# Weight tiles moved by 64 bytes, three loads on another queue, and another order at the end of an encoder block

## The chip, the cores and the metric

The kernel runs on one core of one Trainium2 chip. The metric is the device time of one execution in microseconds (us). TensorE multiplies matrices; VectorE (DVE), ScalarE (ACT) and GpSimd (POOL) work on elements; SyncE (SP) only issues transfers. A PEld row is the load of TensorE's stationary operand, which overlaps the matmul before it.

## The reference

One layer of an encoder on 256 tokens of width 2048, all in float32:

```python
h = _rmsnorm(x, norm1_g)
proj = h @ w_in                      # q: 1536, k: 512, v: 512, u: 512 columns
a = _rmsnorm(_window_attention(q, k, v, sink), attn_out_g)   # 12 heads, 4 kv heads, |t-s| <= 128
f = _rmsnorm(_fourier_mix(u, w_fourier), fourier_out_g)      # Re(DFT2) per group, then a linear map
x = x + jnp.concatenate([a, f], axis=-1) @ w_out
x = x + _conv_ffn(_rmsnorm(x, norm2_g), w_up, dw_w, dw_b, w_down)
return _rmsnorm(x, normf_g)

def _conv_ffn(h, w_up, dw_w, dw_b, w_down):                  # D_FF = 5504
    up = h @ w_up
    gate, val = up[..., :D_FF], up[..., D_FF:]
    gate = depthwise_conv_3(gate, dw_w) + dw_b
    return (jax.nn.gelu(gate, approximate=False) * val) @ w_down
```

## The kernel before

**Products in three parts.** Every large product is computed from numbers split in two: `hi` is the operand rounded to the type float32r, `lo` is what the rounding left. A product is hi x hi + hi x lo + lo x hi, each a float32r matmul that adds into the same PSUM bank. Weights come from memory whole, as units of 128 partitions x 2048 numbers (1 MB), into `raw`; ScalarE makes `hi` from it (L143) and VectorE makes `lo` (L144). `raw`, `hi` and `lo` have three buffers each, used in turn.

**Two kinds of unit.** In `moving_weights` (L282 to L284) the activations are the stationary operand and the weights move, 512 columns at a time: activation-high with `hi`, activation-low with `hi`, activation-high with `lo`. It is used for u and v (`ps_u`, `ps_v`), the output projection (`ps_a`, `ps_ff`) and the down-projection (`ps_d`, and `ps_e` for the last group). One unit has 24 such matmuls. In `still_weights` (L293, L294) the weights are stationary: a block of `hi` meets the tokens' high and low parts together (512 columns), and a block of `lo` the high parts alone (256 columns). It is used for q and k (16 units) and for the up-projection (`ps_gate`, `ps_val`, 86 units). One unit has 16 such pairs.

**The order.** The program is an order written out by hand. u comes first, then v, q and k with the attention of earlier heads woven in, the output projection, and then the feed-forward part: groups of eight up units (four gate, four value), with a group of four down units behind each but the first. `step(i)` splits the unit two ahead while unit i is multiplied; a split ends by issuing the load of the unit three ahead on SP's queue, where it waits until its `raw` buffer is free.

**Where the tiles lie.** A tile begins at the same byte of every partition. By the sizes of the tiles in the pools, in the order in which they are made, the tokens' parts (`hT`, later `hU`) begin at bytes that are 96 modulo 512; `raw`, `hi` and `lo` (8192 bytes each) at 288; `cat` and `act`, the activations of the output and down products, at 288; the attention's `v_hi` and `v_lo` at 448 and its `pt` at 192. A block of 128 stationary columns is 512 bytes of a partition, and all offsets within these tiles are multiples of 512, so these residues hold for every operand.

**The start.** Tokens come transposed as eight tiles `xT`. SP issues the loads in order: the first 256 columns of tokens, the first quarter of weight unit 0, the next 256 columns, the second quarter, the next 512 columns, the third and fourth quarter, and so on (L168 for tokens, L121 for weights). ScalarE's queue issues only the small `vec` (L176), which the first conversion of tokens (L235, then L236 on VectorE) needs too.

**The end.** The last down group has three blocks and is done product by product (`ps_e`): column block c of four, row block b of two. `last_post` adds a product to the running sum `xs` on VectorE (L833), squares it on ScalarE with a running total (L819) and, for c below 3, multiplies it by the final gain on POOL (L836). When all four of a row block are there, `most_of` and `last_scale` form its scale (VectorE L843, L845, L850; POOL L854), and `finish` writes four outputs: c = 0 and 1 on ScalarE (L869), c = 3 (L863) and c = 2 (L867) on VectorE, each with an output transfer on SP's queue (L870). The last product (3, 1) is done in two halves of 256 columns (L941 to L943); `most_of` of row block 1 stands between them.

Of the kernel before, what the change touches and what calls it, by code (L numbers as in the profile page):

```python
# [8 lines left out]
F32 = mybir.dt.float32  # L9
F32R = mybir.dt.float32r  # L10
AF = mybir.ActivationFunctionType
ALU = mybir.AluOpType

P = 128
D = 2048
S = 256
# [36 lines left out]
FF_GROUPS = [list(range(g * 4, min(g * 4 + 4, NF))) for g in range((NF + 3) // 4)]  # L53
# [3 lines left out]
def block_kernel(  # L57
# [17 lines left out]
    nc = tc.nc  # L75
# [3 lines left out]
    wp = ctx.enter_context(tc.tile_pool(name="wp", bufs=1))  # L79
# [3 lines left out]
    def f32(ap):  # L83
        return ap.bitcast(F32)

    def bank(pool, name):
        return pool.tile([P, 512], F32, tag=pool.name, name=name)
# [24 lines left out]
    raws, halves = {}, {}  # L112

    def load(i, pieces=1):
        if i < len(units) and i not in raws:
            src, n = units[i]
            raws[i] = wp.tile([P, 2048], F32, tag="raw", name=f"raw{i}", bufs=RAW)
            m = n // pieces
            for p in range(pieces):
                s = slice(p * m, (p + 1) * m)  # L120
                nc.sync.dma_start(raws[i][:, s], src[:, s])  # L121
                yield
# [6 lines left out]
    def split_parts(i, pieces):  # L129
        if i >= len(units):  # L130
            return
        n = units[i][1]
        raw = raws[i]
        hi = wp.tile([P, 2048], F32R, tag="hi", name=f"hi{i}", bufs=3)
        lo = wp.tile([P, 2048], F32R, tag="lo", name=f"lo{i}", bufs=3)
        halves[i] = (hi, lo)
        m = n // pieces
        for p in range(pieces):
            s = slice(p * m, (p + 1) * m)
            if i == 0 and p == 0:  # L140
                nc.vector.tensor_copy(hi[:, s], raw[:, s])
            else:
                nc.scalar.activation(hi[:, s], raw[:, s], AF.Copy)  # L143
            nc.vector.tensor_tensor(lo[:, s], raw[:, s], f32(hi[:, s]), ALU.subtract)  # L144
            yield
        for _ in load(i + RAW):
            pass
        load_more(i + RAW)
# [8 lines left out]
    xTc = [cat_pool.tile([P, 512], F32, tag="cat", name=f"xT{c}") for c in range(8)]  # L157
# [6 lines left out]
    rel = cat_pool.tile([P, 512], F32, tag="cat", name="rel")  # L164
    xs = [base.tile([P, 2, 512], F32, tag=f"xs{c}", name=f"xs{c}") for c in range(4)]

    def load_x(c, o=0, n=512):
        nc.sync.dma_start(xTc[c][:, o : o + n], xT[:, c * 512 + o : c * 512 + o + n])  # L168


    warm = base.tile([P, 2], F32, tag="warm", name="warm")
# [2 lines left out]

    first = load(0, 4)
    nc.scalar.dma_start(vec[:, 0:NK], vecs[:, 0:NK])  # L176
    load_x(0, 0, S)
    next(first)
    load_x(0, S, S)
    next(first)  # L180
    load_x(1)
    next(first)
    next(first)
    load_x(2)
    second = load(1, 4)
    next(second)
# [16 lines left out]
    def load_more(i):  # L203

        if i == 4:
            for c in range(2):
                nc.sync.dma_start(xs[c], x[:, :, c * 512 : (c + 1) * 512])
        if i == 5:
            for c in range(2, 4):
                nc.sync.dma_start(xs[c], x[:, :, c * 512 : (c + 1) * 512])  # L210
        if i == 6:
            nc.sync.dma_start(chan, c_chan)
            nc.sync.dma_start(wfs, wf)
            nc.sync.dma_start(pos, c_pos)
        if i == 7:
            nc.sync.dma_start(vec[:, NK:V_N], vecs[:, NK:V_N])
            nc.sync.dma_start(rel, c_rel)
# [8 lines left out]
    ps = bank(dn, "ps_warm")  # L226
# [49 lines left out]
    def moving_weights(hi, lo, n, kk, act, b, ps, first, last, q0=0):  # L276

        for q, k in enumerate(kk, q0):
            ah = act(k)[:, b * P : (b + 1) * P]
            al = act(k)[:, S + b * P : S + (b + 1) * P]  # L280
            wh, wl = hi[:, q * n : (q + 1) * n], lo[:, q * n : (q + 1) * n]
            nc.tensor.matmul(ps, ah, wh, start=first and q == q0, stop=False)  # L282
            nc.tensor.matmul(ps, al, wh, start=False, stop=False)  # L283
            nc.tensor.matmul(  # L284
                ps, ah, wl, start=False, stop=last and q == q0 + len(kk) - 1
            )
# [18 lines left out]
    def step(i, ahead=2):  # L305
        todo, later[:] = list(later), []
        for g in todo:
            next(g, None)
        split(i + ahead)
        for g in todo:  # L310
            for _ in g:
                pass
# [24 lines left out]
    for k in range(NK):  # L337
        c, q = k // 4, k % 4
# [4 lines left out]
        hi, lo = halves[c]  # L343
# [392 lines left out]
    for n, (c, kq) in enumerate(OUT_ORDER):  # L736
        i = N_OUT + n
# [14 lines left out]
        if kq >= 2:  # L752
            part = "a" if kq == 2 else "f"
            ps = ps_a[c] if kq < 3 else ps_a[c, "f"]
            last = c in added
# [15 lines left out]
    gfb = fp.tile([P, D], F32, tag="gfb", name="gfb", bufs=1)  # L771
    nc.gpsimd.dma_start(gfb, normf_g.partition_broadcast(P))
    hT[:] = hT2
    act = {}
# [49 lines left out]
    def down_post(g, c, ps):  # L824
# [2 lines left out]
            nc.vector.tensor_tensor(xb, ps[b], xb, ALU.add)  # L827
        yield

    def last_post(c, b, ps, o=0, n=512, part=None):  # L830

        xb = xs[c][:, b, o : o + n]
        nc.vector.tensor_tensor(xb, ps, xb, ALU.add)  # L833
        square_sum(c, b, c if part is None else part, o, n)
        if c < 3:
            nc.gpsimd.tensor_tensor(  # L836
                xb, xb, gfb[:, c * 512 + o : c * 512 + o + n], ALU.mult
            )

    def most_of(b, n):  # L840

        tot = base.tile([P, 1], F32, tag=f"tot3{b}", name=f"tot3{b}")
        nc.vector.tensor_reduce(tot, ssq3[:, b, 0:n], mybir.AxisListType.X, ALU.add)  # L843
        var = base.tile([P, 1], F32, tag=f"part3{b}", name=f"part3{b}")
        nc.vector.tensor_scalar(var, tot, 1.0 / D, EPS, ALU.mult, ALU.add)  # L845
        return var

    def last_scale(b, n, var):
        v = base.tile([P, 1], F32, tag=f"var3{b}", name=f"var3{b}")
        nc.vector.scalar_tensor_tensor(  # L850
            v, ssq3[:, b, n : n + 1], 1.0 / D, var, ALU.mult, ALU.add
        )
        r = base.tile([P, 1], F32, tag=f"rstd3{b}", name=f"rstd3{b}")
        nc.gpsimd.tensor_tensor(r, v, half_pow[:, 0:1], ALU.pow)  # L854
        return r

    def finish(b, r):
        y = [
            fp.tile([P, 512], F32, tag="act", name=f"y{b}{c}", bufs=12) for c in range(4)
        ]  # L860
        for c in (0, 3, 1, 2):
            if c == 3:
                nc.vector.scalar_tensor_tensor(  # L863
                    y[c], xs[c][:, b, :], r, gfb[:, 1536:2048], ALU.mult, ALU.mult
                )
            elif c == 2:
                nc.vector.tensor_scalar(y[c], xs[c][:, b, :], r, None, ALU.mult)  # L867
            else:
                nc.scalar.activation(y[c], xs[c][:, b, :], AF.Copy, scale=r)  # L869
            nc.sync.dma_start(  # L870
                out[b * P : (b + 1) * P, c * 512 : (c + 1) * 512], y[c]
            )

    last = len(FF_GROUPS) - 1
    n = 0
    while n < len(ff_units):
        kind, g, j = ff_units[n]
        i = n_front + n
        if n == 0:
            pair = []  # L880
            for q in range(2):
                ps = bank(mm, f"ps_{ff_units[q][0]}{j}")
# [16 lines left out]
        hi, lo = halves.pop(i)  # L899
        if kind == "down" and g == last:  # L900
            break
        if kind == "down":
            ps = [bank(dn, f"ps_d{g}{j}{b}") for b in range(2)]
# [4 lines left out]
        else:  # L908
            ps = bank(mm, f"ps_{kind}{j}")
# [4 lines left out]


    halves[i] = (hi, lo)
    todo = []
    for c, b in [(0, 0), (0, 1), (1, 0), (1, 1), (2, 0), (3, 0), (2, 1), (3, 1)]:
        hi, lo = halves[i + c]
        ps = bank(dn, f"ps_e{c}{b}")  # L920
        if (c, b) != (3, 1):
            moving_weights(hi, lo, 512, FF_GROUPS[last], act.get, b, ps, True, True)
            todo.append((last_post, (c, b, ps)))
        if (c, b) in [(0, 1), (1, 0)]:
            step(i + c)
        if (c, b) != (0, 0):
            for f, a in todo:
                f(*a)
            todo = []
        if (c, b) == (3, 0):  # L930
            r3 = last_scale(0, 3, most_of(0, 3))
        if (c, b) == (2, 1):
            finish(0, r3)
    for p in range(2):
        ps = bank(dn, f"ps_e31{p}")
        for q, k in enumerate(FF_GROUPS[last]):
            o = q * 512 + p * 256
            ah, al = act[k][:, P:S], act[k][:, S + P : 2 * S]
            wh, wl = hi[:, o : o + 256], lo[:, o : o + 256]
            end = q == len(FF_GROUPS[last]) - 1  # L940
            nc.tensor.matmul(ps[:, 0:256], ah, wh, start=q == 0, stop=False)  # L941
            nc.tensor.matmul(ps[:, 0:256], al, wh, start=False, stop=False)
            nc.tensor.matmul(ps[:, 0:256], ah, wl, start=False, stop=end)  # L943
        last_post(3, 1, ps[:, 0:256], p * 256, 256, 3 + p)
        if p == 0:
            var = most_of(1, 4)
    finish(1, last_scale(1, 4, var))


def _layout(inp):  # L950
# [90 lines left out]
```

## Time and profile before

| What | Value |
|---|---|
| Median of three runs | 990.43 us (990.28 to 990.92) |
| The profiled execution | 989.97 us |
| Its span, first to last instruction | 988.2 us |
| TensorE busy with matmuls | 977.0 us, 5185 matmuls |
| VectorE, ScalarE busy | 696.1 and 466.5 us |
| First and last matmul of the program's own work | start 4.80 and 978.58 us |
| Bytes moved | 186.42 MB, mean 189 GB/s |

A row of the timeline has start, duration, engine, line, operation, output and inputs, shape and count; in brackets stands how long the engine was idle before it and what ended that. A row of groups ends with the busy time in us, the mean duration in ns, and the idle time before. Matmuls are pipelined: a matmul's own duration is longer than the time to the start of the next, so paces are read from starts.

### The profile page before, as it was taken

How to read it: one execution, taken by the hardware profiler on the slowest of the kernel's cores; microseconds unless marked ns; L12 is line 12 of the kernel's file. 1: busy time of each engine (PE TensorE's matmuls, PEld its weight loads, DVE VectorE, ACT ScalarE, POOL GpSimd, SP SyncE). 2: the span in 40 equal slices, each digit the busy share in tenths (PEclk: the TensorE clock that was granted, in tenths of full speed). 3: DMA queues.
4: the chain of work that ended last, by engine and by line, in shares of the span. 5: the costliest groups of instructions: out<-in, count | busy, mean ns of one | idle time of the engine just before them, and what ended most of it. 6: DMA issues, size and time to landing. Idle time of an engine off the chain costs nothing.

```text
span 988.2 us, 12858 instructions
## 1 busy us (share of the span) xinstructions
PE 977.0 (99%) x5185; PEld 838.2 (85%) x5185; DVE 696.1 (70%) x935; ACT 466.5 (47%) x587; POOL 23.6 (2%) x35
## 2 busy tenths in 40 slices
PE   9999999999999999999999999999999999999996
PEld 7788898888888888888888888888888888888885
DVE  6658877575687776767767767777677677676764
ACT  6756666544454434444434444344344343443434
POOL 0000000000000000000000000000000000000003
PEclk9999999999999999999999999999999999999999
DMA  9844443445545555464555555555545455555542
GB/s 330 341 178 153 148 165 134 171 170 205 221 170 178 204 178 206 172 213 171 191 192 180 204 182 201 184 196 177 210 170 208 175 192 192 178 206 190 193 128 86
DMA packets 30091, 186.42 MB, mean 189 GB/s; under 512 B 3408, under 2 KB 3920, under 8 KB 9040
## 3 DMA queue, kind: packets, MB, share of 16 engines
q1 hardware_dynamic: 29744, 184.54, 52.9%
q8 instruction: 41, 0.67, 0.3%
q0 software_dynamic: 144, 1.05, 0.3%
q14 instruction: 18, 0.15, 0.0%
q10 hardware_dynamic: 144, 0.01, 0.0%
HBM read 183.49 MB, written 2.10 MB: 188 GB/s over the span
## 4 chain that ended last, share of the span: by engine, by line
PE 98%; DMA 1%; issue 0%; SPq 0%; ACT 0%; POOL 0%; DVE 0%; ACTq 0%; POOLq 0%
PE ps_gate L293 16%; PE ps_val L293 16%; PE ps_val L294 8%; PE ps_gate L294 8%; PE ps_d L284 7%; PE ps_d L283 7%; PE ps_d L282 7%; PE ps_q L293 5%; PE ps_q L294 2%; PE ps_a L284 2%; PE ps_a L282 2%; PE ps_a L283 2%; PE ps_k L293 2%; PE ps_o L642 1%; PE ps_s L570 1%; PE ps_k L294 1%
## 5 line engine op out<-in xcount | busy, mean ns | idle before, releaser
L144 DVE TENSOR_TENSOR lo<-raw,hi 128x2048 fp32r<-128x2048 f32 (+3 forms) x178 | 388.4, 2182 | 97.7 <-ACT hi L143 97.7
L143 ACT ACTIVATE hi<-raw 128x2048 fp32r<-128x2048 f32 (+3 forms) x177 | 324.3, 1832 | 166.6 <-PE ps_d L283 106.0
L293 PE MATMUL ps_gate<-hU,hi 128*128 128x512 f32 x688 | 242.6, 394 | 0.0
L293 PE MATMUL ps_val<-hU,hi 128*128 128x512 f32 x688 | 242.6, 394 | 0.0
L294 PE MATMUL ps_val<-hU,lo 128*128 128x256 f32 x688 | 193.0, 281 | 0.0
L294 PE MATMUL ps_gate<-hU,lo 128*128 128x256 f32 x688 | 193.0, 280 | 0.0
L293 PEld LDWEIGHTS ps_val<-hU,hi 128*128 128x128 f32 x688 | 129.4, 188 | 30.1
L293 PEld LDWEIGHTS ps_gate<-hU,hi 128*128 128x128 f32 x688 | 129.4, 188 | 30.0
L294 PEld LDWEIGHTS ps_gate<-hU,lo 128*128 128x128 f32 x688 | 128.9, 187 | 0.4
L294 PEld LDWEIGHTS ps_val<-hU,lo 128*128 128x128 f32 x688 | 128.9, 187 | 0.0
L284 PE MATMUL ps_d<-lo,act 128*128 128x512 f32 x320 | 124.6, 389 | 0.0
L283 PE MATMUL ps_d<-hi,act 128*128 128x512 f32 x320 | 124.6, 389 | 0.0
L282 PE MATMUL ps_d<-hi,act 128*128 128x512 f32 x320 | 124.5, 389 | 0.0
L780 ACT ACTIVATE ft_g<-ps_gate 128x256 f32<-128x256 f32 x43 | 16.5, 384 | 134.2 <-PE ps_gate L294 134.2
L827 DVE TENSOR_TENSOR xs<-ps_d,xs 128x512 f32<-128x512 f32 x80 | 54.5, 687 | 25.7 <-PE ps_d L284 25.7
L282 PEld LDWEIGHTS ps_d<-hi,act 128*128 128x128 f32 x320 | 60.1, 188 | 12.6
L284 PEld LDWEIGHTS ps_d<-lo,act 128*128 128x128 f32 x320 | 60.1, 188 | 12.5
L283 PEld LDWEIGHTS ps_d<-hi,act 128*128 128x128 f32 x320 | 60.1, 188 | 12.2
L293 PE MATMUL ps_q<-hT,hi 128*128 128x512 f32 x192 | 68.5, 397 | 0.0
L780 ACT ACTIVATE ft_v<-ps_val 128x256 f32<-128x256 f32 x43 | 16.5, 384 | 95.5 <-PE ps_val L294 95.5
L782 DVE TENSOR_TENSOR fa_g<-ps_gate,ft_g 128x256 f32<-128x256 f32 x43 | 18.2, 424 | 55.3 <-ACT ft_g L780 55.3
L294 PE MATMUL ps_q<-hT,lo 128*128 128x256 f32 x192 | 54.0, 281 | 0.0
(175 smaller groups left out, 1036.1 us busy)
## 6 DMA issues: line engine op xcount, KB each, us to landing
raw<-in_w_up SPq DMA_DIRECT2D x86, 1024.0 KB, 4.8
raw<-in_w_down SPq DMA_DIRECT2D x40, 1024.0 KB, 4.7
raw<-in_w_in SPq DMA_DIRECT2D x21, 1024.0 KB, 4.9
raw<-in_w_out SPq DMA_DIRECT2D x16, 1024.0 KB, 4.8
raw<-in_w_down_last SPq DMA_DIRECT2D x4, 768.0 KB, 4.2
raw<-in_w_in SPq DMA_DIRECT2D x8, 256.0 KB, 5.7
xs<-in_x SPq DMA_DIRECT2D x4, 512.0 KB, 10.8
out_y<-y SPq DMA_DIRECT2D x8, 256.0 KB, 2.5
```

The source lines that it names most:

```text
L143: nc.scalar.activation(hi[:, s], raw[:, s], AF.Copy)
L144: nc.vector.tensor_tensor(lo[:, s], raw[:, s], f32(hi[:, s]), ALU.subtract)
L282: nc.tensor.matmul(ps, ah, wh, start=first and q == q0, stop=False)
L283: nc.tensor.matmul(ps, al, wh, start=False, stop=False)
L284: nc.tensor.matmul(ps, ah, wl, start=False, stop=last and q == q0 + len(kk) - 1)
L293: nc.tensor.matmul(ps, hi[:, s], h, start=k == 0, stop=False)
L294: nc.tensor.matmul(ps[:, 0:S], lo[:, s], h[:, 0:S], start=False, stop=k == NK - 1)
L570: nc.tensor.matmul(ps[:, b * S : (b + 1) * S], qT[:, qo + b * P : qo + (b + 1) * P], kT[:, ko : ko + S], start=n == 0, stop=n == 2,)
L642: nc.tensor.matmul(ps[:, 0:S], v[:, sb, g * HD : (g + 1) * HD], pt[q][:, sb * S : (sb + 1) * S], start=sb == 0 and n == 0, stop=sb == 1 an ...
L780: nc.scalar.activation(tmp, ps[:, S : 2 * S], AF.Copy)
L782: nc.vector.tensor_tensor(add, ps[:, 0:S], tmp, ALU.add)
L827: nc.vector.tensor_tensor(xb, ps[b], xb, ALU.add)
```

## The change

It has three parts.

1. Before the first `hi` tile a tile of 16 numbers (64 bytes) is allocated, and before the first `lo` tile one of 112 numbers (448 bytes). Nothing writes or reads them. `hi` then begins at 352 modulo 512 and `lo`, 512 bytes further on than before, again at 288. All pools behind it move by 512 bytes.
2. The first three token loads are issued from ScalarE's queue, behind `vec`. SP's queue then begins with the four quarters of weight unit 0.
3. The last sums: the multiplication by the gain becomes a function of its own, `gain`, so that for the product (2, 1) it can stand behind the first three outputs of row block 0. `finish` becomes a generator: three outputs of row block 0 are made before the last product, the fourth between its halves. Its output c = 1 is made on POOL instead of ScalarE. `most_of` of row block 1 moves behind the second half's sum.

```diff
+        if not halves and i == 0:
+            wp.tile([P, 16], F32, tag="room_hi", name="room_hi")
         hi = wp.tile([P, 2048], F32R, tag="hi", name=f"hi{i}", bufs=3)
+        if not halves and i == 0:
+            wp.tile([P, 112], F32, tag="room_lo", name="room_lo")
         lo = wp.tile([P, 2048], F32R, tag="lo", name=f"lo{i}", bufs=3)
...
-    def load_x(c, o=0, n=512):
-        nc.sync.dma_start(xTc[c][:, o : o + n], xT[:, c * 512 + o : c * 512 + o + n])
+    def load_x(c, o=0, n=512, queue=None):
+        (queue or nc.sync).dma_start(xTc[c][:, o : o + n], xT[:, c * 512 + o : c * 512 + o + n])
...
     nc.scalar.dma_start(vec[:, 0:NK], vecs[:, 0:NK])
-    load_x(0, 0, S)
-    next(first)
-    load_x(0, S, S)
-    next(first)
-    load_x(1)
-    next(first)
-    next(first)
+    load_x(0, 0, S, nc.scalar)
+    load_x(0, S, S, nc.scalar)
+    load_x(1, queue=nc.scalar)
+    for _ in first:
+        pass
     load_x(2)
...
+    def gain(c, b):
+        xb = xs[c][:, b, :]
+        nc.gpsimd.tensor_tensor(xb, xb, gfb[:, c * 512 : (c + 1) * 512], ALU.mult)
+
     def last_post(c, b, ps, o=0, n=512, part=None):
...
         square_sum(c, b, c if part is None else part, o, n)
-        if c < 3:
-            nc.gpsimd.tensor_tensor(
-                xb, xb, gfb[:, c * 512 + o : c * 512 + o + n], ALU.mult
-            )
...
             elif c == 2:
                 nc.vector.tensor_scalar(y[c], xs[c][:, b, :], r, None, ALU.mult)
+            elif c == 1 and b == 0:
+                nc.gpsimd.tensor_scalar(y[c], xs[c][:, b, :], r, 1.0, ALU.mult, ALU.mult)
             else:
                 nc.scalar.activation(y[c], xs[c][:, b, :], AF.Copy, scale=r)
             nc.sync.dma_start(
                 out[b * P : (b + 1) * P, c * 512 : (c + 1) * 512], y[c]
             )
+            if c != 2 or b:
+                yield
...
+    r3 = last_scale(0, 3, most_of(0, 3))
+    last_post(2, 1, last_product(2, 1))
+    outs = finish(0, r3)
+    for _ in range(3):
+        next(outs)
+    gain(2, 1)
+    hi, lo = halves[i + 3]
     for p in range(2):
         ps = bank(dn, f"ps_e31{p}")
...
         last_post(3, 1, ps[:, 0:256], p * 256, 256, 3 + p)
         if p == 0:
-            var = most_of(1, 4)
-    finish(1, last_scale(1, 4, var))
+            for _ in outs:
+                pass
+    for _ in finish(1, last_scale(1, 4, most_of(1, 4))):
+        pass
```

More of the change, by code (lines that the diff above doesn't have):

```diff
@@ L916, in block_kernel, with last_product @@
     halves[i] = (hi, lo)
-    todo = []
-    for c, b in [(0, 0), (0, 1), (1, 0), (1, 1), (2, 0), (3, 0), (2, 1), (3, 1)]:
+    def last_product(c, b):
         hi, lo = halves[i + c]
         ps = bank(dn, f"ps_e{c}{b}")
[L921 to L933, printed above, removed]
+        moving_weights(hi, lo, 512, FF_GROUPS[last], act.get, b, ps, True, True)
+        return ps
+    held_ps = last_product(0, 0)
+    ps = last_product(0, 1)
+    step(i)
+    last_post(0, 0, held_ps)
+    last_post(0, 1, ps)
+    gain(0, 0)
+    gain(0, 1)
+    ps = last_product(1, 0)
+    step(i + 1)
+    last_post(1, 0, ps)
+    gain(1, 0)
+    for c, b in [(1, 1), (2, 0), (3, 0)]:
+        last_post(c, b, last_product(c, b))
+        if c < 3:
+            gain(c, b)
+    r3 = last_scale(0, 3, most_of(0, 3))
[5 more added lines that the diff above has]
+    hi, lo = halves[i + 3]
     for p in range(2):
```

## Prediction

> **What bounds the kernel now.** I read the page's head and its chain first, then the groups of instructions, then single stretches of the trace.
>
> The head of the page, the granted clock in its second part, and the chain by engine:
>
> ```profile
> span 988.2 us, 12858 instructions
> PE 977.0 (99%) x5185; PEld 838.2 (85%) x5185; DVE 696.1 (70%) x935; ACT 466.5 (47%) x587; POOL 23.6 (2%) x35
> PEclk9999999999999999999999999999999999999999
> PE 98%; DMA 1%; issue 0%; SPq 0%; ACT 0%; POOL 0%; DVE 0%; ACTq 0%; POOLq 0%
> ```
>
> TensorE is on the chain for 98% of the span at full granted clock. Time can leave in three ways only: fewer ns between the starts of two matmuls, an earlier start, or a shorter tail after the last matmul. The change touches each. A busy PE hides the first, so I measured stretches that begin and end with a matmul's start (stretch, PE busy, instructions that touch it, clock, DMA):
>
> ```profile
> 12.60:18.20 5.60, 5.60 (x25) 1.00 1.06 403
> 297.07:302.73 5.66, 5.66 (x35) 1.00 0.52 190
> 453.00:458.58 5.58, 5.58 (x34) 1.00 0.52 188
> 951.39:956.83 5.44, 5.44 (x25) 1.00 0.62 187
> 82.42:88.06 5.64, 5.64 (x34) 1.00 0.52 186
> 420.04:425.51 5.47, 5.47 (x26) 1.00 0.56 193
> 94.85:95.56 0.71, 0.71 (x8) 1.00 0.00 0
> ```
>
> The counts include instructions that overlap an edge. The first and fourth stretches hold 24 matmuls 512 wide, with weights moving (`ps_u`, `ps_d`): 233.3 and 226.7 ns each, the same shape. The second, third and fifth hold 16 pairs of a 512-wide and a 256-wide matmul over still weights (two up units and a `ps_k` unit): 354, 349 and 353 ns a pair. The sixth is the first down unit behind an up stage; it takes 5.47 where a later one takes 5.44. The last is six 256-wide `ps_o` matmuls, 118 ns each.
>
> For a flat 256-wide interval there is the last product, 18 matmuls, first and last:
>
> ```profile
> 976.55 0.28 PE L941 MATMUL ps_e<-hi,act 128*128 128x256 f32 x1
> 978.58 0.28 PE L943 MATMUL ps_e<-lo,act 128*128 128x256 f32 x1
> ```
>
> 17 intervals in 2.03 us are 119.4 ns. A flat pair is therefore 226.7 + 119.4 = 346.1 ns, and a flat up unit 16 of them, 5.54 us.
>
> So equal work runs at two or three paces, though clock and instructions are the same. What differs is where the two streams that TensorE reads begin, the moving operand of one matmul and the load for the next. By the tiles' places modulo 512 the distance (load less moving) is 0 in the down stage, 320 in `ps_u`, 192 in the up, q and k units and 256 in `ps_o`. Flat are 0 and 256; 192 and 320 have the extra time. But the pace also moves at equal places (354 in the 18 units of the first two up groups, 349 later), so it depends on how the streams fell into step, too.
>
> **Part 1: high parts 64 bytes on.** It removes and adds no instruction: two tiles that nobody writes. The low parts, tokens and activations keep their places modulo 512. In up, q and k units the load of a high part, made during the 256-wide matmul, goes from distance 192 to 256; the load of a low part stays at 192. In `ps_u` and `ps_v` two of three go from 320 to 256. In the down and output products, two of three go from 0 to 448, which no row shows.
>
> The whole extra in the still-weight units: 68 later up units x (5.58 - 5.54) = 2.7 us, 18 early ones x (5.66 - 5.54) = 2.2, 16 q and k units x (5.64 - 5.54) = 1.6; together 6.5. One of the two loads in each pair moves to a distance seen flat, so I take half, 3.3 us, between 0 and 6.5. For the 8 units of `ps_u` and `ps_v` the extra is 8 x (5.60 - 5.44) = 1.3 us; I take 0 of it, since that stretch is held by data (below). For the down and output products the nearest rows are the flat one and the first one: between 0 and 58.6 units (40 `ps_d`, 16 output, 63 matmuls of `ps_e`) x 24 x 2/3 x 6.7 ns = 6.3 us worse. I take 0, because the 5.47 against 5.44 shows that this stage settles by itself after a bad beginning, and every third load still stands at distance 0. That is the weakest step.
>
> VectorE and ScalarE I cost at nothing: 128x2048 parts take 2290 and 1912 ns, 128x1536 ones 1758 and 1486, so 1.04 and 0.83 ns per further column at both sizes, and nothing in these rows depends on the place:
>
> ```profile
> L144 DVE TENSOR_TENSOR lo<-raw,hi 128x2048 fp32r<-128x2048 f32 x162 | 371.0, 2290 | 88.8 <-ACT hi L143 88.8
> L143 ACT ACTIVATE hi<-raw 128x2048 fp32r<-128x2048 f32 x162 | 309.7, 1912 | 150.6 <-PE ps_d L283 94.6 <-issue 27.4 <-PE ps_a L283 13.4
> L144 DVE TENSOR_TENSOR lo<-raw,hi 128x1536 fp32r<-128x1536 f32 x4 | 7.0, 1758 | 4.1 <-ACT hi L143 4.1
> L143 ACT ACTIVATE hi<-raw 128x1536 fp32r<-128x1536 f32 x4 | 5.9, 1486 | 11.4 <-PE ps_d L283 11.4
> ```
>
> **Part 2: the first tokens through ScalarE's queue.** The issues at the start, ScalarE's and TensorE's waits, and the two that matter later:
>
> ```profile
> 0.74 0.39 SPq L168 DMA_DIRECT2D xT<-in_xT  x1
> 0.91 0.38 ACTq L176 DMA_DIRECT2D vec<-in_vecs  x1
> 1.20 0.42 SPq L121 DMA_DIRECT2D raw<-in_w_in  x1
> 2.60 0.43 SPq L168 DMA_DIRECT2D xT<-in_xT  x1
> 3.08 0.91 SPq L121 DMA_DIRECT2D raw<-in_w_in  x2
> 3.28 0.51 ACT L235 ACTIVATE hT<-xT,vec 128x256 fp32r<-128x256 f32 x1 [1.04 <-DMA vec<-in_vecs]
> 8.76 0.63 ACT L143 ACTIVATE hi<-raw 128x512 fp32r<-128x512 f32 x1 [1.02 <-DMA raw<-in_w_in]
> 9.45 0.50 PE L282 MATMUL ps_u<-hi,hT 128*128 128x512 f32 x1 [0.27 <-ACT hi L143]
> 22.82 1.23 DVE L144 TENSOR_TENSOR lo<-raw,hi 128x1024 fp32r<-128x1024 f32 x1 [1.50 <-ACT hi L143]
> 24.27 0.39 PE L284 MATMUL ps_u<-lo,hT 128*128 128x512 f32 x1
> 9.45:24.20 14.75, 14.75 (x62) 11.60 (x63) 11.52 (x20) 11.47 (x21) 0.00 (x0) 1.00 1.03 402
> ```
>
> Three issues leave SP, so the third weight piece goes out at about 1.7 instead of 3.08, and all SP issues behind it come up to 1.4 us earlier. On ScalarE the three stand behind that of `vec`, at about 1.3, 1.7 and 2.1; the first conversion L235, queued behind them, waits for `vec` until 3.28 anyway. Its tokens go out 0.56 later and may arrive after that, so the first matmul may start up to 0.56 later; TensorE's idle time before 9.45, when that third piece arrived, covers this. From 9.45 on TensorE never waits, with DMA at 1.03 of its engines. The next deadline is low part 3: ready at 22.82 + 1.23 = 24.05, used at 24.27. Unless the bytes themselves come sooner, 0.2 us can be gained. I take 0.2, between 1.4 (everything moves up with the issues) and -0.6. By the Trainium skill, DMA: Bandwidth & Descriptors, section "Issuing engines are not separate DMA queues", a second issuing engine saves issue time alone. The 1.03 agrees with that, and by it the sum would also hold 0.2.
>
> **Part 3: order of the last sums and outputs.**
>
> ```profile
> 977.36 0.74 DVE L863 SCALAR_TENSOR_TENSOR y<-xs,rstd,gfb 128x512 f32<-128x512 f32 x1
> 978.02 0.48 DVE L867 TENSOR_SCALAR y<-xs,rstd 128x512 f32<-128x512 f32 x1
> 979.92 0.16 DVE L843 TENSOR_REDUCE tot<-ssq 128x1 f32<-128x4 f32 x1 [1.09 <-ACT junkc L819]
> 980.18 0.41 DVE L833 TENSOR_TENSOR xs<-ps_e,xs 128x256 f32<-128x256 f32 x1
> 978.17 1.32 ACT L869 ACTIVATE y<-xs,rstd 128x512 f32<-128x512 f32 x2
> 978.34 1.29 POOL L836 TENSOR_TENSOR xs<-xs,gfb 128x512 f32<-128x512 f32 x1 [1.17 <-ACT junkc L819]
> 982.06 1.34 ACT L869 ACTIVATE y<-xs,rstd 128x512 f32<-128x512 f32 x2 [0.86 <-POOL rstd L854]
> 140.14 0.74 POOL L412 TENSOR_TENSOR sq_a<-sq_a,sq 128x256 f32<-128x256 f32 x1 [6.75 <-ACT sq L411]
> 140.40 0.76 DVE L236 SCALAR_TENSOR_TENSOR qT<-add_q,qT 128x256 fp32r<-128x256 f32 x1 [0.82 <-ACT qT L235]
> L236 DVE SCALAR_TENSOR_TENSOR cat<-ps_o,vec,cat 128x256 fp32r<-128x256 f32 x12 | 5.8, 482 | 6.5 <-ACT cat L235 6.5
> ```
>
> The last matmul ends at 978.58 + 0.28 = 978.86, but the addition that takes it starts at 980.18, behind L843, which waits for a square that ScalarE does only after two outputs (1.32). The change sends one of these to POOL and puts L843 behind the addition. Without other waits the addition starts at about 978.9 to 979.0, and scale, outputs and their eight issues come 1.2 us sooner. A price stands against it: POOL's new output (nearest row: L836, 1.29 for 128x512) runs beside L863, and the moved `gain` beside L867. L236 shows it: 0.76 us beside POOL's 0.74, where 482 ns is usual, so POOL's work costs VectorE up to its own length; two such meetings before the addition could eat all 1.2 us. I take 0.6, between 0 and 1.2. By the Trainium skill, SBUF — State Buffer, section "Who interferes with whom", an operation of VectorE with two inputs in SBUF contends with a GpSimd one that reads SBUF, and one of them blocks; 0.76 against 0.48 agrees, and it speaks against this part.
>
> **The sum.** 3.3 + 0.2 + 0.6 = 4.1 us. The profiled execution took 989.97 us around a span of 988.2, 0.46 below the median of 990.43; from the median, 990.43 - 4.1 = 986.3.
>
> **The rivals.**
> A. The place does nothing. For it: the pace differs at equal places (5.66 and 5.58). Against: 5.60 and 5.44 for equal shapes never mix. Time: 990.43 - 0.8 = 989.6. By the Trainium skill, TensorE: Matmul & The Clock Gate, section "Step-by-step: what each phase is for", loading the next weights takes no read bandwidth from the running matmul, as each has its own port. By that rule the time is 989.6 too; that the 5.60 and 5.44 stretches differ speaks against it here.
> B, on the other side. The down and output products lose their step: two thirds of their matmuls take 233 instead of 227 ns. For it: 448, like the bad 192 and 320, is an odd multiple of 64, and only distance 0 was seen flat for 512-wide matmuls. Against: the settling. Time: 990.43 - 0.8 + 6.3 = 995.9 without a gain in the up units, 992.6 with it. It decides once over a third of these products is lost.
> C. Part 3 turns into waiting on POOL and the start comes 0.6 later, the place doing nothing: 990.43 + 0.6 = 991.0.
>
> **How the numbers follow.** Forecast 0.50, A 0.20, B 0.27, C 0.03. What a measurement of this kernel can tell from no change is about 0.2%, 2 us: below 988.4 counts as faster, above 992.4 as slower. The forecast is faster (0.50), A and C are the same (0.23), B is slower (0.27). The forecast's own range is 983 to 988.4, its lower end the whole extra of the up units with the full tail. The range for 8 in 10 is 983 to 994.8; it reaches into B until a full loss alone is left out.
>
> **What would show it.** Right: an up unit of 5.54 to 5.58 everywhere and down units still at 5.44; the last addition under 0.6 us behind the last matmul; SP's third weight piece out before 2. Wrong: a down unit near 5.55 (B); up units unchanged (A); VectorE's L863 over 1 us and the addition still near 980. If the pace follows neither distance nor step but some other stream, part 1 is wrong in either direction.

## The result, and the profile after

The changed kernel takes 997.13 us (median; 995.63 to 998.88) where the kernel before, in the same measurement, takes 990.48: a ratio of 1.0067, with an interval of 1.0054 to 1.0080. It is slower by 6.65 us. The profiled execution took 997.06 us around a span of 995.2, 7.0 above the span before.

The head of the page:

```profile
span 995.2 us, 12861 instructions
PE 983.1 (99%) x5185; PEld 838.4 (84%) x5185; DVE 697.4 (70%) x935; ACT 466.0 (47%) x586; POOL 24.3 (2%) x36
PE 98%; DMA 0%; ACT 0%; issue 0%; DVE 0%; POOL 0%; ACTq 0%; POOLq 0%
```

TensorE does as many matmuls as before and is still 98% of the chain; it is busy 6.1 us longer. So the same matmuls start further apart. Stretches from a matmul's start to another's show where. A row gives the stretch, its length, the busy time of PE, PEld, VectorE, ScalarE and POOL (in brackets the instructions that touch it), and at the end the granted clock, the share of the transfer engines and GB/s. First of the kernel before: an output unit, then whole stages, namely 14 up units of the first two groups, 8 up units of a later group and 4 down units.

```profile
233.81:239.25 5.44, 5.44 (x26) 4.50 (x25) 3.70 (x3) 1.92 (x2) 0.00 (x0) 1.00 0.51 197
274.38:353.61 79.23, 79.23 (x452) 68.96 (x451) 62.66 (x84) 37.78 (x46) 0.00 (x0) 1.00 0.53 186
375.38:420.04 44.66, 44.66 (x257) 39.11 (x256) 32.41 (x41) 19.80 (x22) 0.00 (x0) 1.00 0.53 187
420.04:441.83 21.79, 21.79 (x98) 18.02 (x97) 15.21 (x15) 8.28 (x7) 0.00 (x0) 1.00 0.58 196
```

And of the changed kernel: a unit of `ps_u`, an early and a late up unit, a down unit and an output unit, then the same three stages.

```profile
14.15:19.70 5.55, 5.55 (x26) 4.56 (x25) 3.37 (x5) 3.41 (x6) 0.00 (x0) 1.00 1.03 414
293.76:299.36 5.60, 5.60 (x35) 4.88 (x33) 5.28 (x8) 2.62 (x3) 0.00 (x0) 1.00 0.74 275
450.16:455.76 5.60, 5.60 (x35) 4.88 (x33) 4.43 (x6) 2.62 (x3) 0.00 (x0) 1.00 0.43 171
952.71:958.26 5.55, 5.55 (x25) 4.50 (x24) 3.75 (x4) 1.93 (x1) 0.00 (x0) 1.00 0.55 157
251.13:256.73 5.60, 5.60 (x26) 4.50 (x24) 3.87 (x2) 2.92 (x2) 0.00 (x0) 1.00 0.21 53
276.87:355.36 78.49, 78.49 (x451) 68.42 (x450) 62.65 (x84) 37.83 (x46) 0.00 (x0) 1.00 0.53 188
377.55:422.36 44.81, 44.81 (x257) 39.03 (x256) 32.44 (x41) 19.81 (x22) 0.00 (x0) 1.00 0.53 186
422.36:444.55 22.19, 22.19 (x98) 18.01 (x97) 15.26 (x15) 8.29 (x7) 0.00 (x0) 1.00 0.56 193
```

The clock (1.00) and the share of the transfers are as before. Down units go from 5.44 to 5.55, the output unit shown from 5.44 to 5.60. All up units now take 5.60, where there were two paces, 5.66 early and 5.58 later. A down stage is 22.19 - 21.79 = 0.40 us longer; there are ten, 4.0 us. The last down group (`ps_e`) begins 7.1 us later than before, at 969.36 instead of 962.27.

VectorE's and ScalarE's parts cost what they did, 2290 and 1912 ns before:

```profile
L149 DVE TENSOR_TENSOR lo<-raw,hi 128x2048 fp32r<-128x2048 f32 x162 | 371.0, 2290 | 89.4 <-ACT hi L148 89.4
L148 ACT ACTIVATE hi<-raw 128x2048 fp32r<-128x2048 f32 x162 | 310.3, 1915 | 155.5 <-PE ps_d L286 97.4 <-issue 28.2 <-PE ps_a L286 14.3
```

The start, from the timeline (start, duration, engine); the last two rows are stretches again, the first nine matmuls and a part of them:

```profile
0.73 1.81 SPq L121 DMA_DIRECT2D raw<-in_w_in  x4
0.98 3.86 PE L231 MATMUL ps_warm<-ones 128*128 128x128 f32 x20 [0.98 <-POOL ones L223]
1.31 0.93 ACTq L173 DMA_DIRECT2D xT<-in_xT  x2
5.42 0.51 ACT L238 ACTIVATE hT<-xT,vec 128x256 fp32r<-128x256 f32 x1 [3.20 <-DMA xT<-in_xT]
6.93 0.47 PE L285 MATMUL ps_u<-hi,hT 128*128 128x512 f32 x1 [2.09 <-DVE hi L146]
6.93:10.72 3.79, 3.79 (x10) 2.75 (x11) 3.75 (x8) 3.54 (x9) 0.00 (x0) 0.55 1.02 365
7.29:10.71 3.42, 3.42 (x9) 2.48 (x8) 3.38 (x8) 3.17 (x8) 0.00 (x0) 0.50 1.01 362
```

The first tokens go out at 1.31, behind four weight pieces that SP issues from 0.73 on, and ScalarE waits for them until 5.42; before, its first conversion started at 3.28. The first matmul starts at 6.93 instead of 4.80, and the first nine run at a mean clock of 0.55: full speed until 7.29, then half speed until 10.71.

The end:

```profile
984.73 0.97 DVE L866 SCALAR_TENSOR_TENSOR y<-xs,rstd,gfb 128x512 f32<-128x512 f32 x1
985.71 1.28 POOL L835 TENSOR_TENSOR xs<-xs,gfb 128x512 f32<-128x512 f32 x1 [0.55 <-ACT junkc L822]
985.93 0.28 PE L962 MATMUL ps_e<-lo,act 128*128 128x256 f32 x1
985.95 1.31 DVE L870 TENSOR_SCALAR y<-xs,rstd 128x512 f32<-128x512 f32 x1
987.19 0.41 DVE L840 TENSOR_TENSOR xs<-ps_e,xs 128x256 f32<-128x256 f32 x1
```

From the start of the last matmul to the end it is 995.2 - 985.93 = 9.27 us, before 988.2 - 978.58 = 9.62. The output L870 (L867 before) takes 1.31 beside POOL's multiplication, where it took 0.48, and the last addition waits for it.

### The profile page after: what moved, and what is told of

Read it like the earlier page. It is cut to its first block, busy times and chain, and to the rows that moved or that the text cites. A ratio compares the mean times of both kernels' runs of the same rounds, so it can differ in the third digit from the quotient of the medians.

```text
span 995.2 us, 12861 instructions
## 1 busy us (share of the span) xinstructions
PE 983.1 (99%) x5185; PEld 838.4 (84%) x5185; DVE 697.4 (70%) x935; ACT 466.0 (47%) x586; POOL 24.3 (2%) x36
## 3 DMA queue, kind: packets, MB, share of 16 engines
q0 software_dynamic: 144, 1.05, 0.3%
## 4 chain that ended last, share of the span: by engine, by line
PE 98%; DMA 0%; ACT 0%; issue 0%; DVE 0%; POOL 0%; ACTq 0%; POOLq 0%
PE ps_gate L296 16%; PE ps_val L296 16%; PE ps_gate L297 8%; PE ps_val L297 8%; PE ps_d L287 8%; PE ps_d L286 7%; PE ps_d L285 7%; PE ps_q L296 5%; PE ps_a L286 2%; PE ps_a L285 2%; PE ps_q L297 2%; PE ps_a L287 2%; PE ps_k L296 1%; PE ps_o L645 1%; PE ps_s L573 1%; PE ps_u L287 1%
## 5 line engine op out<-in xcount | busy, mean ns | idle before, releaser
L287 PE MATMUL ps_d<-lo,act 128*128 128x512 f32 x320 | 127.0, 397 | 0.0
```

The costliest lines, as they stand in the source:

```text
L287: nc.tensor.matmul(ps, ah, wl, start=False, stop=last and q == q0 + len(kk) - 1)
```

## The experiments

Theory P: the pace of the products goes by the places of the tiles, and part 1 carries the loss. Rival S: the pace is what the streams fell into by their history, and the late start changed that.

**Each part alone.** Part 1 alone (the two unused tiles):

```diff
+        if not halves and i == 0:
+            wp.tile([P, 16], F32, tag="room_hi", name="room_hi")
         hi = wp.tile([P, 2048], F32R, tag="hi", name=f"hi{i}", bufs=3)
+        if not halves and i == 0:
+            wp.tile([P, 112], F32, tag="room_lo", name="room_lo")
```

> The kernel before with the two unused tiles alone. Theory P (the loss is in the pace of the products whose weights move, set by the places): down unit 5.55 instead of 5.44 us, output unit 5.6 or more instead of about 5.5, up units near 5.60 everywhere; 58.6 units x 0.1 us or a little more, less about 1 us for u and v, so about 995 to 996 us. Rival S (the pace is what the streams fell into by their history, and the late start set it): with the early start of the kernel before, the down unit stays at 5.44 and the time within 2 us of 990.5.

996.87 us, ratio 1.0063 (1.0048 to 1.0078), a little above the 995 to 996 expected: part 1 is the loss. A later up stage and a down stage:

```profile
377.61:422.42 44.81, 44.81 (x258) 39.10 (x256) 32.43 (x41) 19.79 (x22) 0.00 (x0) 1.00 0.53 185
422.42:444.61 22.19, 22.19 (x98) 18.01 (x97) 15.26 (x15) 8.28 (x7) 0.00 (x0) 1.00 0.55 193
```

Both are those of the changed kernel, though this one starts as the kernel before does. So the late start did not set the pace; P holds for the down products.

Part 2 alone (the first tokens on ScalarE's queue):

```diff
-    load_x(0, 0, S)
-    next(first)
+    load_x(0, 0, S, nc.scalar)
...
```

> The kernel before with the first three token loads on ScalarE's queue alone. Theory H (the first tokens arrive late, TensorE then stands idle for about 2 us and runs its first matmuls at half speed): first matmul of ps_u near 6.9 instead of 4.80 us, nine matmuls at about 0.43 us, the end 1 to 2 us later, 991.5 to 992.5 us. Rival (the stretch held by data hides it, as predicted): 990.0 to 990.6 us.

992.02 us, ratio 1.0012 (1.0002 to 1.0021). The ten times stand at two levels: three from 990.47 to 991.09, seven from 991.88 to 992.27. The profiled one is the fastest:

```profile
1.00 4.63 PE L226 MATMUL ps_warm<-ones 128*128 128x128 f32 x20 [1.00 <-POOL ones L218]
7.21 0.47 PE L280 MATMUL ps_u<-hi,hT 128*128 128x512 f32 x1 [1.57 <-DVE hi L141]
```

Here the warm-up lasted until 5.63, TensorE was idle for 1.57 instead of 2.09 us, and the next matmuls start 0.23 us apart, not 0.43. So the late landing is there (7.21), but the half speed is not. The upper level could be executions with the half speed; a later run tests that.

Part 3 alone (the end as in the change):

> The kernel before with the new order of the last sums and outputs alone. From the start of the last matmul to the end of the span: 9.27 us instead of 9.62 if POOL's multiplication by the gain holds up the output L870 (theory C, contention: 1.31 us instead of 0.48), so 990.1 us; 8.4 us and 989.3 us if that meeting was an accident of the profiled execution.

```profile
978.54 1.29 POOL L832 TENSOR_TENSOR xs<-xs,gfb 128x512 f32<-128x512 f32 x1 [0.38 <-ACT junkc L819]
978.78 0.28 PE L959 MATMUL ps_e<-lo,act 128*128 128x256 f32 x1
978.96 1.16 DVE L867 TENSOR_SCALAR y<-xs,rstd 128x512 f32<-128x512 f32 x1
980.04 0.41 DVE L837 TENSOR_TENSOR xs<-ps_e,xs 128x256 f32<-128x256 f32 x1
```

The same meeting again: 1.16 beside 1.29, and 9.27 us from the last matmul's start to the end, as in the changed kernel. The 0.35 us are too little for the times: 990.51, ratio 1.0001 (0.9991 to 1.0010). The up and down stages of this kernel and of part 2 alone are, to 0.02 us, those of the kernel before.

**Without part 1.** The changed kernel less the two unused tiles:

```diff
-        if not halves and i == 0:
-            wp.tile([P, 16], F32, tag="room_hi", name="room_hi")
...
-        if not halves and i == 0:
-            wp.tile([P, 112], F32, tag="room_lo", name="room_lo")
```

> The changed kernel without the two unused tiles: tokens on ScalarE's queue and the new tail. If the parts add up, down stage 21.79 and up stages 44.66 us as before, and the time 990.5 + 1.5 where TensorE's first matmuls run at half speed, less 0.4 for the tail: two levels, near 990.2 and 991.7 us. If the new tail or the new start also cost pace, the stages are longer than before.

991.42 us, ratio 1.0007 (0.9997 to 1.0016); its stages are 44.66 and 21.79 again. Parts 2 and 3 cost nothing in the stages, and together no more than 0.16%. The ten times stand at two levels again, as expected: four from 989.97 to 990.63, six from 991.42 to 992.87. Here the profiled one, 991.51, is of the upper level, and its first matmuls do run at half speed, 0.43 us from start to start:

```profile
7.26 0.77 PE L280 MATMUL ps_u<-hi,hT 128*128 128x512 f32 x1 [1.64 <-ACT hT L233]
8.25 0.63 PE L282 MATMUL ps_u<-lo,hT 128*128 128x512 f32 x1
8.68 0.63 PE L280 MATMUL ps_u<-hi,hT 128*128 128x512 f32 x1
```

**All distances 0.** If distance 0 is flat, as the prediction took from the down units, then moving the tokens' parts so that every large product has it should be a gain:

```diff
+        if c == 0:
+            base.tile([P, 48], F32, tag="room_hT", name="room_hT")
         t = base.tile([P, 4, 512], F32R, tag=f"hT{c}", name=f"hT{c}")
+        if c == 3:
+            base.tile([P, 80], F32, tag="room_hTe", name="room_hTe")
```

> The kernel before with the tokens' parts hT and hU moved by 192 bytes, from 96 to 288 modulo 512 (an unused tile ahead of them, one behind so that all else keeps its place), so that in every large product load and moving operand are at distance 0. Theory P (distance 0 throughout is flat): up and q, k units 5.54, u and v units 5.44, down units 5.44 as before; 6.5 + 1.3 us at most, so 983 to 985 us. Rival S (history, not place): up units still between 5.58 and 5.66, 989 to 992 us.

993.77 us, ratio 1.0030 (1.0018 to 1.0042): slower. Both theories missed. The 14 early up units and a later stage:

```profile
275.24:352.98 77.74, 77.74 (x452) 68.00 (x450) 62.66 (x84) 37.80 (x46) 0.00 (x0) 1.00 0.54 190
374.76:419.97 45.21, 45.21 (x257) 39.23 (x256) 32.43 (x41) 19.80 (x22) 0.00 (x0) 1.00 0.53 184
```

77.74 / 14 = 5.55 us a unit early, 45.21 / 8 = 5.65 later, at the same places. The order is the reverse of that of the kernel before (5.66 and 5.58). What differs is the entry: the early units come behind four small matmuls (`ps_spread`), and their first matmul starts 0.31 us ahead of the second; a later stage comes straight from a down unit, and there it is 0.23. Within a stage the start times repeat one short cycle to its end. So theory E: places allow several cycles, and the entry chooses.

**Another entry.** One small extra matmul ahead of each later up stage, into a bank that the stage overwrites, at equal places and in the kernel before:

```diff
+            if ff_units[n - 1][0] == "down":
+                nc.tensor.matmul(ps[:, 0:16], ones, ones[:, 0:16], start=True, stop=True)
             still_weights(hi, lo, ps, range(NK))
```

> The kernel with all places equal (distance 0), and ahead of each up stage that follows a down stage one small extra matmul of ones, 128x16, into the bank that the stage then overwrites. Theory E (a stage repeats the cycle of start times that it enters with; entered behind other work it takes 5.55 us a unit, entered straight from a down unit 5.65): all later up units 5.55 instead of 5.65, so 70 x 0.098 = 6.9 us less than the 993.8 of equal places alone, and 8 extra matmuls of 0.1 to 0.3 us more: 988 to 989 us. Rival L (what the later stages have beside them, VectorE's, ScalarE's and the transfers' work, makes the difference): 5.65 stays, 994 to 996 us.

> The kernel before with the same extra matmul ahead of each later up stage. Theory E: the later up units take on the pace of its first two up stages, 5.66 instead of 5.58 us, and the time rises by 70 x 0.076 = 5.3 us and 1 to 2 us for the extra matmuls, to about 997. Rival L: 5.58 stays, 991.5 to 992.5 us.

With equal places 988.66 us, ratio 0.9975 (0.9966 to 0.9985), 5.1 less than without the extra matmuls; in the kernel before, 997.54 in a single run. A later up stage of the first and then of the second, from the stage's own first matmul on; the extra one ahead of it takes 0.14 us more:

```profile
374.29:418.75 44.46, 44.46 (x259) 39.20 (x258) 32.42 (x41) 19.66 (x22) 0.00 (x0) 1.00 0.53 187
```

```profile
376.27:421.56 45.29, 45.29 (x259) 39.47 (x258) 32.43 (x41) 19.65 (x22) 0.00 (x0) 1.00 0.52 185
```

45.21 became 44.46, and 44.66 became 45.29, though each has one more matmul ahead of it. What stands beside these stages on VectorE, ScalarE and the queues did not change, so rival L falls; E holds, in both directions as expected.

**The down products' places, two ways.** High and low parts both 64 bytes on, and the low parts alone:

```diff
+        if not halves and i == 0:
+            wp.tile([P, 16], F32, tag="room_hi", name="room_hi")
         hi = wp.tile([P, 2048], F32R, tag="hi", name=f"hi{i}", bufs=3)
         lo = wp.tile([P, 2048], F32R, tag="lo", name=f"lo{i}", bufs=3)
+        if not halves and i == 0:
+            wp.tile([P, 112], F32, tag="room_end", name="room_end")
```

This is the first; in the second the tile of 16 numbers stands between `hi` and `lo`.

> The kernel before with high and low parts 64 bytes on (both at 352 modulo 512, the rest in place). In down and output units all three moving matmuls are then at distance 448, and in the up units both loads at 256. Theory D (each matmul pays for its own distance): the down unit goes beyond the 5.55 us of the changed kernel, to about 5.60 (three thirds of the loss instead of two). Theory U (what costs is that high and low parts lie at unequal distances, so that the step changes three times a block): the down unit is back at 5.44 to 5.46. Up units: 5.54 if 256 is flat, else again one of several paces.

> The kernel before with the low parts alone 64 bytes on: in down and output units one moving matmul of three is at distance 448, two at 0. Theory D: a third of a full loss, so a down unit of about 5.49 us. Theory U: about the 5.55 of the changed kernel, since high and low parts lie as far apart.

Both parts on: 992.14 us in a single run; two up stages that follow each other and a down stage:

```profile
374.19:419.40 45.21, 45.21 (x258) 39.23 (x257) 32.42 (x41) 19.83 (x22) 0.00 (x0) 1.00 0.52 185
441.39:485.77 44.38, 44.38 (x258) 39.12 (x257) 32.44 (x41) 19.85 (x22) 0.00 (x0) 1.00 0.53 188
485.77:507.74 21.97, 21.97 (x98) 18.03 (x97) 15.24 (x15) 8.30 (x7) 0.00 (x0) 1.00 0.57 195
```

Low parts alone on: 985.31 us in a single run, below every time of the kernel before beside it (989.99 to 992.24):

```profile
375.79:419.32 43.53, 43.53 (x257) 38.62 (x256) 32.42 (x41) 19.80 (x22) 0.00 (x0) 1.00 0.54 192
419.32:441.60 22.28, 22.28 (x99) 18.02 (x97) 15.26 (x15) 8.28 (x7) 0.00 (x0) 1.00 0.56 192
```

Matmuls at distance 448, by third of a down unit, and the unit: none 5.45, one third (low) 5.57, two thirds (high) 5.55, all three 5.49. The cost is not in proportion (D falls). Unequal distances come nearer, but they are not all of it, as all three at 448 do not give 5.45 back (U as it stands falls too). In the first of the two kernels the up stages alternate, 45.21 and 44.38 and so on to the end, at the same places and without any added matmul. That fits E, if one stage's cycle sets how the down stage ends, and that the next entry. Its 45.21, and the 77.74 us of its 14 early units, are also those of equal places: distances 0 and 256 gave the same cycles here. In the second the up unit takes 43.53 / 8 = 5.44 us, less than the 5.54 that the prediction thought flat.

**The entry of the down stage.** Part 1 alone, and the small extra matmul ahead of each down stage:

```diff
+            if ff_units[n - 1][0] != "down":
+                nc.tensor.matmul(ps[0][:, 0:16], ones, ones[:, 0:16], start=True, stop=True)
             for b in range(2):
                 moving_weights(hi, lo, 512, FF_GROUPS[g], act.get, b, ps[b], True, True)
```

> The two unused tiles alone, and one small extra matmul of ones ahead of each down stage, into the bank that its first product then overwrites. If the step that the down products lose is one of several cycles, chosen on entry as in the up units, the down stage of four units leaves 22.19 us, towards 21.8 or to a third value; if these places have one pace only, it stays at 22.19 and the extra matmul's 0.1 to 0.3 us.

```profile
421.71:444.12 22.41, 22.41 (x101) 18.24 (x100) 15.26 (x15) 8.29 (x7) 0.00 (x0) 1.00 0.56 190
488.92:511.54 22.62, 22.62 (x101) 18.22 (x99) 15.26 (x15) 8.28 (x7) 0.00 (x0) 1.00 0.56 190
```

The single run takes 999.45 us. The ten stages alternate between 22.41 (22.19 and about 0.2 for the extra matmul) and 22.62, a slower cycle. So these places, too, have more than one cycle. Both that were seen are slower than 21.79; why they alternate is not shown.

**Each kind of unit at its own place.** Only q, k and up units gain by the low parts' shift, and only down and output units lose. A unit's low parts can lie anywhere in its buffer:

```diff
-        lo = wp.tile([P, 2048], F32R, tag="lo", name=f"lo{i}", bufs=3)
+        still = N_QK <= i < N_QK + 16 or (
+            i >= n_front and ff_units[i - n_front][0] != "down"
+        )
+        lo = wp.tile([P, 2176], F32R, tag="lo", name=f"lo{i}", bufs=3)
+        lo = lo[:, 16:2064] if still else lo[:, 0:2048]
```

> The kernel before with the low parts of q, k and up units alone 64 bytes on (each low buffer has 128 spare columns; these units use it from column 16, all others from column 0). If the pace of a kind of unit goes by its own places and the cycle that it enters, up and q, k units are those of the low parts alone on (5.44 us for the later up units, instead of 5.58) and down and output units those of the kernel before (5.45 instead of 5.57): 985.3 - 40 x 0.12 - 16 x 0.11 - 0.3, about 978 to 979 us. If the end of the down stage before decides the cycle of the up stage, the up units can come out at 5.55 to 5.66 instead, and the time at 986 to 993 us.

978.85 us, ratio 0.9878 (0.9863 to 0.9893).

```profile
373.61:417.15 43.54, 43.54 (x257) 38.62 (x256) 32.41 (x41) 19.81 (x22) 0.00 (x0) 1.00 0.55 191
417.15:438.94 21.79, 21.79 (x99) 18.02 (x98) 15.21 (x15) 8.28 (x7) 0.00 (x0) 1.00 0.59 196
```

The fast up stage and the fast down stage together: the paces add up as expected.

**The end without the meeting.** Part 3, with the gain for (2, 1) on VectorE behind the last sums:

```diff
-    gain(2, 1)
...
+    var = most_of(1, 4)
+    xb = xs[2][:, 1, :]
+    nc.vector.tensor_tensor(xb, xb, gfb[:, 1024:1536], ALU.mult)
+    for _ in finish(1, last_scale(1, 4, var)):
```

> The new order of the last sums alone, with the multiplication by the gain for product (2, 1) on VectorE behind the last sums instead of on POOL beside L870. Theory C (POOL's operation holds VectorE's output up): that output takes 0.48 instead of 1.16 to 1.31 us, the last addition starts about 0.3 to 0.5 us behind the last matmul's end instead of about 1, and the time from the start of the last matmul to the end is about 8.5 us instead of 9.2. Rival: VectorE is slow there for another reason, and 9.2 stays or grows by the 0.7 of the multiplication.

```profile
979.64 0.28 PE L958 MATMUL ps_e<-lo,act 128*128 128x256 f32 x1
979.82 0.47 DVE L867 TENSOR_SCALAR y<-xs,rstd 128x512 f32<-128x512 f32 x1
980.21 0.41 DVE L837 TENSOR_TENSOR xs<-ps_e,xs 128x256 f32<-128x256 f32 x1
```

L867 is back at 0.47, and from the last matmul's start to the end it is 8.7 us: contention it was. The expected 8.5 is missed by 0.2, of which 0.13 is the scale's L850, which now waits behind the moved multiplication: it starts 1.18 us behind the start of the last addition, against 1.05 in part 3 alone. (990.13 us, one run, says nothing on half a microsecond.)

**A longer warm-up.** Part 2 alone with more matmuls of ones:

```diff
-WARM = 10
+WARM = 16
```

> The kernel before with the first tokens on ScalarE's queue and 16 instead of 10 warm-up matmuls, so that TensorE works until about 6 us. Theory G (the 992.1 us of most executions with these tokens on ScalarE's queue is the half speed of the first nine or so matmuls behind TensorE's idle 2 us): no half speed any more, all executions near 990.5 to 991. Rival (the late landing alone): both levels stay, most executions near 992.

```profile
1.00 5.72 PE L226 MATMUL ps_warm<-ones 128*128 128x128 f32 x32 [1.00 <-POOL ones L218]
7.38 0.47 PE L280 MATMUL ps_u<-hi,hT 128*128 128x512 f32 x1 [0.66 <-DVE hi L141]
```

990.81 us, ratio 1.0002 (0.9993 to 1.0012), all ten between 990.42 and 991.20: the upper level is gone, though the first matmul starts no sooner. So part 2's price is the half speed of the first matmuls, which it has in some executions and not in others; the late landing by itself costs no more than 0.12%.

**Both gains.** The last two ideas that helped, each unit kind at its place and the end without the meeting, with the tokens as before:

> Both together: low parts of q, k and up units 64 bytes on, and the new order of the last sums with the gain for (2, 1) on VectorE; tokens as before. About 1.1 us below place_by_kind if the tail's gain is real: 977 to 978 us.

977.27 us, ratio 0.9865 (0.9849 to 0.9882): 1.35% faster than the kernel before, 2.0% faster than the changed one. Its early up units still take the slower cycle (78.48 us for 14, 5.61 each); another entry there was not tried.

## Why the prediction was wrong

**The forecast** was 986.3 us, with a range of 983 to 994.8. The time is 997.13, outside it. What happened is rival B in its form without a gain in the up units, 995.9, and part 2's loss on top.

**The step that failed: "I take 0, because the 5.47 against 5.44 shows that this stage settles by itself".** The stage does settle, but into the cycle that its places allow, and at distances 448 and 0 that is a slower one. Measured: ten down stages x 0.40 = 4.0 us, 16 output units 2.2 us (summed start to start, part 1 alone against before), `ps_e` 0.3: 6.5 us, just above the upper bound of 6.3 that stood there. The settling that was seen was at distance 0, and it was evidence on that place alone. The third load still at distance 0 did not help.

**Part 1, up, q and k units: 3.3 taken, about 0 measured**, by three changes that happen to cancel. The early 14 units gain 79.23 - 78.49 = 0.7 us, the 70 later ones lose 1.3 (8 stages of 0.15 and a last one of 0.1), q and k gain 0.6. (The early groups hold 16 units, not the 18 that the prediction counted.) The failed step is "one of the two loads in each pair moves to a distance seen flat, so I take half": 256 was flat for 256-wide `ps_o` matmuls alone, and a pair's pace is not the sum of its halves. Nor was 346.1 ns the flat pair, as 43.53 us for 128 pairs is 340.1. `ps_u` and `ps_v` did go faster, 5.60 to 5.55 and 0.4 us over all of `ps_v`, for which 0 was taken.

**VectorE and ScalarE at nothing:** right.

**Part 2: a gain of 0.2 taken, a loss measured.** SP's third piece did go out before 2, as expected, but the tokens became usable 2.1 us later, not 0.56: they went out beside four weight pieces on the same transfer engines, whose busy share was 0.88 from 2.20 to 5.42. "TensorE's idle time before 9.45 [...] covers this" held for the waiting, as the longer warm-up shows, and failed for what comes of the waiting: TensorE's first matmuls ran at half speed behind it. By the Trainium skill, DMA: Bandwidth & Descriptors, section "Issuing engines are not separate DMA queues", transfers of all issuing engines interleave on the same 16 engines, and the 5.42 agrees; the prediction used this rule for the gain and not against the tokens. Price: 1.0 to 1.5 us, by 991.42 less 990.76 and the 0.35 that part 3 gives back, and by 992.02 less 990.50 alone.

**Part 3: 0.6 taken, 0.35 measured** in the traces; the run times do not resolve it. The mechanism, POOL's work beside VectorE's, was right, and of the two meetings named L870 cost more (0.83) than L866 (0.23). (The prediction set its 0.76 against the 0.48 of another form of L236; the same form usually takes 0.42, so POOL's work added 0.34 there.)

**The sum.** 6.5 - 0.0 - 0.4 + (1.0 to 1.5) - 0.35 gives 6.75 to 7.25 us; measured are 6.65 between the medians and 7.0 between the spans.

By the Trainium skill, TensorE: Matmul & The Clock Gate, section "Step-by-step: what each phase is for", loading the next weights takes no read bandwidth from the running matmul. By that alone the places would not matter. Stages of 43.54, 44.66 and 45.21 us with the same instructions, told apart by places and entry alone, say that they do; that it is the loads that hold up the matmuls is not shown.

What stays open is the mechanism below: which access of the two streams waits for which. The runs show that places set the possible cycles and the entry one of them; they do not show why a cycle has its length, and no rule here says beforehand which place is fast.

## What to carry to other kernels

When TensorE bounds, measure start to start for a whole stage, not busy time: the same matmuls were up to 4% apart here (43.54 against 45.29 us) by where the tiles begin, in shifts of 64 and 192 bytes, and by what ran just before. Do not carry the pace of one product over to another or to half a pair; try a few places for each kind of product apart, as one shift that helps the one can harm the next. And a transfer that is moved to another queue still shares the engines with those that now go out ahead of it.

## What the runs showed that was not expected

- A stage's pace repeats to the nanosecond from run to run: the later up stages are 44.66 us and the down stages between them 21.79 in the kernel before and in five variants that leave the places alone, whatever their starts.
- At the same places and clock, with both parts moved, an up stage takes 45.21 and 44.38 us in turn; at equal places one 128x16 matmul ahead turns 45.21 into 44.46.
- In the changed kernel the granted clock fell to half at 7.29, when matmuls had run again for 0.36 us, and was full again at 10.71. In the 3.41 us before 7.29 TensorE had been idle for 2.09. By the Trainium skill, TensorE: Matmul & The Clock Gate, section "Part 1: The HAM clock gate", the clock goes by free-running windows of about 3.4 us and halves after an idle one; the 3.42 us at half speed agree, and here the idle time did not have to fill a window. The length of the idle time alone does not decide: behind 1.64 us (without part 1) the first matmuls ran at half speed, behind 1.57 (part 2 alone) they did not. How the windows lay in these two is not shown.
- An output with a single tensor input (L870, L867) is held up by POOL as well: 1.16 to 1.31 us instead of 0.48.
